# A decoder trunk's attention layer: low parts of weights on VectorE, small multiplications on GpSimd, one transfer for a piece of compression's weights

## The chip, the cores and the metric

The kernel runs on one core of a Trainium2 chip. Its engines run side by side: TensorE (PE: matrix products, and PEld: its weight loads), VectorE (DVE), ScalarE (ACT), GpSimd (POOL), and SyncE (SP), which here only issues transfers. Sixteen DMA engines move data between the chip's memory (HBM) and the engines' buffer (SBUF); products are summed in eight banks of PSUM. The metric is the time of one execution in microseconds (us), the median of several.

## The reference

Two layers over 256 tokens of 1024 channels, float32 throughout. The change lies in the second layer, between the two feed-forward parts:

```python
def compress(kv_raw, pe, w1, w2):
    idx = jnp.arange(n_cmp)[:, None] * D_CMP + jnp.arange(L_CMP)[None, :]      # blocks of 32 tokens, step 16
    blocks = kv_raw[:, idx] + pe[None, None, :, None, :]
    blocks = blocks.transpose(0, 1, 3, 2, 4).reshape(bsz, n_cmp, N_KV_GROUPS, L_CMP * HEAD_DIM)
    return jax.nn.silu(blocks @ w1) @ w2                                       # w1: 2048 x 256

# x: stream after layer 0
kv = (rms_norm(x, kv_norm) @ w_kv).reshape(bsz, seq, 6, 4, 64)   # compressed, selected and window K and V
k_cmp, v_cmp = compress(kv[:, :, 0], ...), compress(kv[:, :, 1], ...)
qg = rms_norm(x, b_norm) @ w_qg                                  # 16 heads' queries, and gates
o = g0 * attend(q, k_cmp, v_cmp) + g1 * attend(q, k_slc, v_slc) + g2 * attend(q, k_win, v_win)
x = x + o @ w_o
x = x + swiglu(rms_norm(x, f_norm)) 
```

Each of the three attentions is a softmax with a distance bias per head. The first layer (a gated short convolution and a feed-forward part) and the last feed-forward part are not touched.

## The kernel before

Tokens lie along the free dimension, channels along the 128 partitions. For accuracy each operand of a product is split into a *high part* (rounded to fp32r) and a *low part* (the rest): `h_...` and `l_...`; a product is then two or three products. So each piece of weights, 128 × 1024, goes through three steps in `split_weights`: SyncE issues its transfer into a raw buffer `w_...` (L316 or L318), ScalarE or GpSimd copies it to `h_...` (L320, L322), VectorE or GpSimd subtracts to `l_...` (L326). The table `CFG["units"]` says for each piece who does it: `False` is ScalarE for the high part and VectorE for the low part; `True` gives the low part to GpSimd; `'both'` gives each half of the low part; `'hi'` gives the high part to GpSimd; `'all'` gives it both parts.

From the attention layer on there are four raw buffers (tag `raw`), so the transfer of a piece waits until the piece four places before it is split; and three buffers for the parts of each of two rings (`a`, `r`).

The pieces of the attention layer are named K (keys; K0 and K1 are what will be compressed), Q, V, Y (`w1` of the compression: Y00 to Y03 for keys, Y10 to Y13 for values), GP (gates) and O (output). `CFG["plan"]` is the order in which the layer is written: `K2a` is the product with that piece, `CB0` builds the blocks `xc` of keys to compress from `cf0` (L767, L768), `Y00` multiplies them with a piece of `w1` into `py` (L779, L780), `J` and `t` are the hidden layer and its transposition, `ck` the compressed keys, `S0` the scores of a head (`sa`, `sb`, L964), and `A`, `r` ask for one more piece ahead. A marker `|n` sets which engines keep the written order from there on; elsewhere a scheduler places instructions by its own costs. From `|4` on no engine is bound, from `|5` TensorE is:

```python
Q0b K4b A Y00 A A A Y10 R0 B1 Y11 A V0 A M0 Y01 A Y02 V1 Y03 J0 Y12 A r A KR4 KR2 A |5 Y13 J1 t0 GP Q1a t1 ck
V2 P0 S0 M1 GR G0 B2 A B3 S1 B4 A C0 S2 V3 G1 B5 N cv A Q1b Q2a r r S3 G2 T0 Q2b R1 ...
```

Products of Y: a piece holds four blocks of 128 rows (two token offsets of 64 channels each) by 256 columns. `CFG["eng"]` names an engine for small steps: `r` scales a head's reciprocal sums by its gates (L988), `c` subtracts a maximum from the compressed scores `cb` (L998), `s` and `m` scale the compressed sums and probabilities (L1008, L1009), `q` splits the queries (first letter high part, second low part; `a`, `d`, `p` are ScalarE, VectorE, GpSimd).

Of the kernel before, what the change touches and what calls it, by code (L numbers as in the profile page):

```python
# [24 lines left out]
DH = 64  # L25
# [24 lines left out]
         'b7': 'p',  # L50
         'b8': 'a',
         'b9': 'p',
         'c0': 'd',
         'c1': 'd',
         'c2': 'd',
         'c3': 'd',
         'c4': 'p',
         'c5': 'p',
         'c6': 'd',
         'c7': 'p',  # L60
         'g000': 'p',
         'g001': 'p',
# [53 lines left out]
         'g900': 'p',  # L116
         'g901': 'p',
         'g910': 'a',
         'm0': 'd',
         'm1': 'd',  # L120
         'm2': 'p',
         'm3': 'p',
         'm4': 'd',
         'm5': 'p',
         'm6': 'p',
         'm7': 'd',
         'q00': 'ap',
         'q01': 'ad',
         'q10': 'pd',
         'q11': 'ad',  # L130
         'q20': 'pd',
         'q21': 'ad',
         'q30': 'pd',
         'q31': 'pp',
         'r0': 'p',
         'r1': 'd',
         'r10': 'd',
         'r11': 'p',
         'r12': 'd',
         'r13': 'p',  # L140
         'r14': 'd',
         'r15': 'p',
         'r4': 'd',
         'r5': 'p',
         'r6': 'd',
         'r7': 'd',
         'r8': 'd',
         'r9': 'p',
         's0': 'p',
         's1': 'd',  # L150
         's2': 'd',
         's3': 'p',
         's4': 'd',
         's5': 'p',
         's6': 'p',
         's7': 'd',
         'x0': 'ap',
         'x1': 'ap',
         'x2': 'pp',
# [9 lines left out]
 'qdma': 0,  # L169
 'sq': {'n1': 0, 'n3': 1},  # L170
 'units': {'GP': ('a', False),
           'K0a': ('a', 'all'),
           'K0b': ('a', False),
           'K1a': ('r', False),
           'K1b': ('r', 'both'),
           'K2a': ('a', 'both'),
           'K2b': ('a', False),
           'K4a': ('a', 'both'),
           'K4b': ('r', 'both'),
           'O0a': ('r', False),  # L180
# [3 lines left out]
           'O2a': ('r', False),
           'O2b': ('r', 'both'),
           'O3a': ('a', 'both'),
           'O3b': ('r', True),
           'O4a': ('r', True),
           'O4b': ('r', True),
           'O5a': ('r', 'both'),  # L190
           'O5b': ('r', True),
           'O6a': ('r', 'both'),
           'O6b': ('a', 'all'),
           'O7a': ('a', 'both'),
           'O7b': ('r', True),
           'Q0a': ('a', 'both'),
           'Q0b': ('r', 'both'),
           'Q1a': ('a', False),
           'Q1b': ('r', 'both'),
           'Q2a': ('a', False),  # L200
           'Q2b': ('a', True),
           'Q3a': ('a', True),
           'Q3b': ('a', True),
           'V0': ('a', True),
           'V1': ('r', 'both'),
           'V2': ('r', False),
           'V3': ('a', True),
           'Y00': ('a', True),
           'Y01': ('a', 'both'),
           'Y02': ('r', False),  # L210
           'Y03': ('a', False),
           'Y10': ('r', True),
           'Y11': ('a', True),
           'Y12': ('a', 'both'),
           'Y13': ('r', 'both')}}
CFG["plan"] = """
H4 K2a H7 K0a A H5 A A K0b A K1a H2 A H0 B0 H1 |4 A K1b H3 NR H6 A A A I NS CR0 CR1 A CB0 K2b Q0a K4a CB1 A
Q0b K4b A Y00 A A A Y10 R0 B1 Y11 A V0 A M0 Y01 A Y02 V1 Y03 J0 Y12 A r A KR4 KR2 A |5 Y13 J1 t0 GP Q1a t1 ck
# [9 lines left out]
def trunk(ctx: ExitStack, tc: tile.TileContext, a):  # L228
    nc = tc.nc
# [32 lines left out]
    def bank(name, kind="short", hold=False):  # L262

        b = min((b for b in ring[kind] if b not in held.values()), key=used.get)
        touch(b)
        if hold:
            held[name] = b
        return psum.tile([P, 512], F32, tag=f"b{b}", name=name)
# [7 lines left out]
    def f(ap):  # L276
        return ap.bitcast(F32)
# [24 lines left out]
    def split_weights(src, name, cols, ring, pool):  # L302
        if (name[0], ring) in spare:
            w, hi, lo = spare.pop((name[0], ring))
        else:
            if phase["name"] == "attention" or name[0] == "O" or name[:2] == "kv":
                w = wp.tile([P, 1024], F32, tag="raw", name=f"w_{name}", bufs=4)
            else:
                w = phase["pool"].tile([P, 1024], F32, tag="raw", name=f"w_{name}", bufs=12)
            hi, lo = (wp.tile([P, 1024], F32R, tag=ring + hl, name=f"{hl}_{name}", bufs=3) for hl in "hl")  # L310
            if name[0] == "O":
                spare[name[0], ring] = [x[:, cols:] for x in (w, hi, lo)]
            w, hi, lo = (x[:, :cols] for x in (w, hi, lo))
        if isinstance(src, list):
            for r, part in enumerate(src):
                nc.sync.dma_start(out=w[r * DH:(r + 1) * DH].rearrange("p (two x) -> p two x", two=2), in_=part)  # L316
        else:
            nc.sync.dma_start(out=w, in_=src)  # L318
        if pool in ("hi", "all"):
            nc.gpsimd.tensor_copy(hi, w)  # L320
        else:
            nc.scalar.activation(hi, w, AF.Copy)  # L322
        cut = {False: 0, True: cols, "both": cols // 2, "hi": 0, "all": cols}[pool]
        for eng, c0, c1 in ((nc.gpsimd, 0, cut), (nc.vector, cut, cols)):
            if c0 < c1:
                eng.tensor_tensor(out=lo[:, c0:c1], in0=w[:, c0:c1], in1=f(hi[:, c0:c1]), op=ALU.subtract)  # L326
        return hi, lo

    class Stream:
# [3 lines left out]
        def ahead(self, n=3):  # L333
            while len(self.ready) < n:
                u = next(self.todo, None)
                if not u:
                    return
                self.ready.append(split_weights(u[1], u[0], u[2], u[4] if len(u) > 4 else self.ring, u[3]))
# [22 lines left out]
    takes = {}  # L361
# [5 lines left out]
    for q in range(4):  # L367
        for st in range(2):

            w1 = a["w1"][st].rearrange("(two d) x -> d two x", two=2)  # L370
            takes[f"Y{st}{q}"] = [w1[:, :, (4 * half + q) * 512:(4 * half + q + 1) * 512] for half in range(2)], 1024
        takes[f"V{q}"] = a["w_v"][q], 1024
    takes["GP"] = a["w_g"], KC * 48

# [395 lines left out]
    def cmp_piece(st, q):  # L770
        if q == 0:
            py[st] = bank(f"py{st}", hold=True)
        wh, wl = wa.take()
        for i in range(4):

            lp = 4 * q + 2 * (i % 2) + i // 2
            first, last = q == 0 and i == 0, q == 3 and i == 3
            x = xc[st].rearrange("p hl g (n l) -> p l (hl g) n", l=16)[:, lp]
            nc.tensor.matmul(py[st][:, :256], x, wh[:, i * 256:(i + 1) * 256], start=first, stop=False)  # L779
            nc.tensor.matmul(py[st][:, :256], x, wl[:, i * 256:(i + 1) * 256], start=False, stop=last)  # L780
# [316 lines left out]
    def hid(st):  # L1097
# [6 lines left out]
          "Q": lambda x: q_piece(int(x[0]), "ab".index(x[1])), "R": lambda x: q_rest(int(x)),  # L1104
          "P": lambda x: q_split(int(x)), "M": lambda x: cmp_second(int(x)),
          "Y": lambda x: cmp_piece(int(x[0]), int(x[1])), "J": lambda x: cmp_hidden(int(x)),
          "V": lambda x: value_piece(int(x)), "N": lambda x: value_rest(), "GP": lambda x: gate_proj(),
          "GR": lambda x: gate_rest(), "B": lambda x: bias(int(x)), "t": lambda x: hid(int(x)),
# [156 lines left out]
```

## Time and profile before

| | before |
|---|---|
| median of 3 runs | 662.78 us (661.78 to 668.63) |
| the profiled execution | 669.47 us, its span 667.6 us |
| TensorE busy | 628.9 us (94%) |
| VectorE busy | 490.3 us (73%) |
| ScalarE busy | 379.1 us (57%) |
| GpSimd busy | 326.0 us (49%) |
| mean granted clock of TensorE | 0.976 of full speed |
| moved by DMA | 109.52 MB, mean 164 GB/s |

The attention layer runs from about 280 to 475 us of the span. A busy share is a mean over stages with different limits; what a change is worth is read from the stage in which it lies.

### The profile page before, as it was taken

To read this page: it belongs to the slowest core of one execution; us is meant where nothing else is said; L and a number is where in the kernel's file an instruction comes from. 1 tells how busy PE (TensorE), PEld (TensorE's weight loads), DVE (VectorE), ACT (ScalarE), POOL (GpSimd) and SP (SyncE) were. 2 spreads that over 40 slices of the span, in tenths; PEclk is the share of its full clock that TensorE was granted. 3 is DMA by queue.
4 is the path that set the end of the run, shared out by engine and by line. 5 is a ranking of instruction groups with operands and counts; after the bars stand their busy time and mean duration, and the time that the engine had idled before them with its cause. 6 is when DMAs were issued, how large, how long until landed. Compare 5 with 4: busy or idle time off the path is not lost.

```text
span 667.6 us, 11200 instructions
## 1 busy us (share of the span) xinstructions
PE 628.9 (94%) x4094; PEld 573.1 (86%) x4094; DVE 490.3 (73%) x773; ACT 379.1 (57%) x744; POOL 326.0 (49%) x285
## 2 busy tenths in 40 slices
PE   7999999999999999879959979999899999999995
PEld 7999998899999999769949869889788888888884
DVE  5688777866666666769996998787986666666664
ACT  7544457545555544437655758997766554444543
POOL 3163225754444444547564675757845444444422
PEclk9999999999999999989989889999899999999998
DMA  8978672655555550031767520003975555555001
GB/s 299 356 303 256 214 245 83 220 190 189 189 187 187 183 179 23 1 127 54 194 171 233 166 95 2 17 17 130 407 291 182 186 179 180 187 186 188 1 1 63
DMA packets 37383, 109.52 MB, mean 164 GB/s; under 512 B 5712, under 2 KB 8144, under 8 KB 37328
## 3 DMA queue, kind: packets, MB, share of 16 engines
q1 hardware_dynamic: 37184, 108.55, 48.0%
q8 instruction: 32, 0.52, 0.3%
q10 hardware_dynamic: 144, 0.26, 0.1%
q14 instruction: 23, 0.19, 0.1%
HBM read 107.22 MB, written 1.05 MB: 162 GB/s over the span
## 4 chain that ended last, share of the span: by engine, by line
PE 75%; DVE 14%; issue 3%; POOL 3%; ACT 3%; DMA 1%; SPq 0%; POOLq 0%; DVEq 0%; ACTq 0%
PE pgu L654 22%; PE pgu L656 11%; PE acc L397 4%; PE acc L398 4%; PE acc L396 4%; PE acc L716 3%; PE acc L715 3%; PE acc L714 3%; DVE n L451 2%; PE pcv L398 2%; PE pcv L397 2%; PE pcv L396 2%; DVE xc L768 1%; POOL l_d L326 1%; PE po L1051 1%
## 5 line engine op out<-in xcount | busy, mean ns | idle before, releaser
L654 PE MATMUL pgu<-n,h_gu 128*128 128x512 f32 x704 | 250.6, 398 | 4.1 <-DVE n L451 2.5
L656 PE MATMUL pgu<-n,l_gu 128*128 128x256 f32 x704 | 197.3, 281 | 0.4 <-DVE l_gu L326 0.4
L654 PEld LDWEIGHTS pgu<-n,h_gu 128*128 128x128 f32 x704 | 132.7, 189 | 35.1 <-DVE n L451 2.5
L326 DVE TENSOR_TENSOR l_gu<-w_gu,h_gu 128x1024 fp32r<-128x1024 f32 x88 | 117.1, 1332 | 26.5 <-ACT h_gu L322 25.4
L656 PEld LDWEIGHTS pgu<-n,l_gu 128*128 128x128 f32 x704 | 133.4, 190 | 2.2 <-DVE l_gu L326 1.1
L667 POOL TENSOR_TENSOR gu<-gu,n_rbc 128x512 f32<-128x512 f32 x40 | 53.2, 1332 | 166.0 <-DVE gu L663 145.1
L672 DVE TENSOR_TENSOR av<-sg,gu 128x256 f32<-128x256 f32 x44 | 79.5, 1809 | 67.9 <-ACT sg L670 67.9
L326 POOL TENSOR_TENSOR l_d<-w_d,h_d 128x1024 fp32r<-128x1024 f32 x43 | 105.2, 2450 | 7.7 <-ACT h_d L322 7.2
L322 ACT ACTIVATE h_gu<-w_gu 128x1024 fp32r<-128x1024 f32 x88 | 92.7, 1053 | 7.1 <-PE pb L397 3.5
L418 ACT ACTIVATE a_h<-av 128x256 fp32r<-128x256 f32 x44 | 18.3, 417 | 78.9 <-DVE av L672 78.9
L322 ACT ACTIVATE h_d<-w_d 128x1024 fp32r<-128x1024 f32 x44 | 46.8, 1063 | 24.5 <-PE acc L716 20.4
L396 PE MATMUL acc<-a_h,h_d 128*128 128x256 f32 x176 | 50.6, 289 | 5.1 <-ACT a_h L418 5.1
L670 ACT ACTIVATE sg<-gu 128x256 f32<-128x256 f32 x44 | 18.2, 417 | 62.1 <-POOL gu L667 52.5
L397 PE MATMUL acc<-a_l,h_d 128*128 128x256 f32 x176 | 50.8, 289 | 0.7 <-DVE a_l L421 0.7
L398 PE MATMUL acc<-a_h,l_d 128*128 128x256 f32 x176 | 50.5, 287 | 0.0
L326 DVE TENSOR_TENSOR l_in<-w_in,h_in 128x768 fp32r<-128x768 f32 (+1 forms) x33 | 38.8, 1187 | 10.7 <-ACT h_in L322 9.5
L322 ACT ACTIVATE h_in<-w_in 128x768 fp32r<-128x768 f32 (+1 forms) x33 | 27.1, 824 | 29.7 <-PE pb L397 20.5
L396 PEld LDWEIGHTS acc<-a_h,h_d 128*128 128x128 f32 x176 | 34.3, 196 | 6.4 <-ACT a_h L418 5.6
L661 ACT ACTIVATE gu<-pgu 128x256 f32<-128x256 f32 x88 | 32.4, 370 | 11.4 <-PE pgu L656 11.4
L398 PE MATMUL pcv<-n,l_in 128*128 128x256 f32 x128 | 36.9, 288 | 1.7 <-DVE l_in L326 1.7
L396 PE MATMUL pcv<-n,h_in 128*128 128x256 f32 x128 | 36.7, 287 | 1.5 <-ACT h_in L322 1.5
L663 DVE TENSOR_TENSOR gu<-pgu,gu 128x256 f32<-128x256 f32 x88 | 36.4, 416 | 1.4 <-ACT gu L661 1.3
(432 smaller groups left out, 1642.1 us busy)
## 6 DMA issues: line engine op xcount, KB each, us to landing
w_gu<-in_w_gu SPq DMA_DIRECT2D x88, 512.0 KB, 4.1
w_d<-in_w_down SPq DMA_DIRECT2D x44, 512.0 KB, 3.4
w_in<-in_w_in SPq DMA_DIRECT2D x31, 384.0 KB, 6.4
w_wo<-in_w_out SPq DMA_DIRECT2D x8, 512.0 KB, 6.7
w_kvY<-in_w SPq DMA_DIRECT2D x16, 256.0 KB, 4.2
w_kvV<-in_w_v SPq DMA_DIRECT2D x4, 512.0 KB, 3.7
h<-in_xT SPq DMA_DIRECT2D x3, 256.0 KB, 5.9
out<-y SPq DMA_DIRECT2D x3, 256.0 KB, 2.3
```

The costliest lines, as they stand in the source:

```text
L322: nc.scalar.activation(hi, w, AF.Copy)
L326: eng.tensor_tensor(out=lo[:, c0:c1], in0=w[:, c0:c1], in1=f(hi[:, c0:c1]), op=ALU.subtract)
L396: nc.tensor.matmul(out, wh, xh, start=start, stop=False, skip_group_check=True)
L397: nc.tensor.matmul(out, wh, xl, start=False, stop=False, skip_group_check=True)
L398: nc.tensor.matmul(out, wl, xh, start=False, stop=stop, skip_group_check=True)
L654: nc.tensor.matmul(ps[j][c], uh[:, cols], x[:, :, k], start=k == 0, stop=False, skip_group_check=True)
L656: nc.tensor.matmul(ps[j][c][:, :S], ul[:, cols], x[:, 0, k], start=False, stop=k == KC - 1, skip_group_check=True)
L661: nc.scalar.activation(gus[j][:, c], ps[j][c][:, S:], AF.Copy)
L663: nc.vector.tensor_tensor(out=gus[j][:, c], in0=ps[j][c][:, :S], in1=gus[j][:, c], op=ALU.add)
L667: (nc.gpsimd if j < NF - 2 else nc.vector).tensor_tensor(out=gu, in0=gu, in1=norm.bc.unsqueeze(1).to_broadcast([P, 2, S]), op=ALU.mult)
L672: nc.vector.tensor_tensor(out=av, in0=sg, in1=gu[:, 1], op=ALU.mult)
L714: nc.tensor.matmul(out, xh, wh, start=start, stop=False, skip_group_check=True)
```

## The change

It has three parts. First, the table `units` gives nearly all low parts of K, Q, V, Y and GP to VectorE and their high parts to ScalarE; most O pieces get `'hi'`, so GpSimd makes the high part and VectorE the low one. Second, the table `eng` gives 21 small steps (five `c`, four `m`, eight `r`, four `s`) from VectorE to GpSimd; q00 and q10 change too. Third, a piece of `w1` comes in one transfer: the rows that a piece takes change (64 of 128 rows of the array, both halves of the columns), and with them the order `lp` in which `cmp_piece` takes its blocks.

```diff
@@ CFG['eng'] @@
-         'c0': 'd',          (c1, c2, c3, c6; m0, m1, m4, m7; r1, r4, r6, r7, r8, r10, r12, r14; s1, s2, s4, s7 alike)
+         'c0': 'p',
-         'q00': 'ap',
+         'q00': 'ad',
-         'q10': 'pd',
+         'q10': 'ad',
@@ CFG['units'] @@
-           'K0a': ('a', 'all'),
+           'K0a': ('a', False),
-           'K1b': ('r', 'both'),          (K2a, K4a, K4b, Q0a, Q0b, Q1b, V1, Y01, Y12, Y13 alike)
+           'K1b': ('r', False),
-           'Y00': ('a', True),            (Q2b, Q3a, Q3b, V0, V3, Y10, Y11 alike)
+           'Y00': ('a', False),
-           'O0b': ('r', 'all'),           (O1a: 'all'; O2a: False; O2b, O3a, O5a, O6a: 'both'; O3b, O4a, O4b, O5b: True)
+           'O0b': ('r', 'hi'),
...
-        if isinstance(src, list):
-            for r, part in enumerate(src):
-                nc.sync.dma_start(out=w[r * DH:(r + 1) * DH].rearrange("p (two x) -> p two x", two=2), in_=part)
-        else:
-            nc.sync.dma_start(out=w, in_=src)
+        nc.sync.dma_start(out=w, in_=src)
...
-            w1 = a["w1"][st].rearrange("(two d) x -> d two x", two=2)
-            takes[f"Y{st}{q}"] = [w1[:, :, (4 * half + q) * 512:(4 * half + q + 1) * 512] for half in range(2)], 1024
+            w1 = a["w1"][st, q % 2 * DH:(q % 2 + 1) * DH].rearrange("d (half x) -> half d x", half=2)
+            takes[f"Y{st}{q}"] = w1[:, :, q // 2 * 1024:(q // 2 + 1) * 1024], 1024
...
-            lp = 4 * q + 2 * (i % 2) + i // 2
+            lp = 8 * (q // 2) + 2 * i + q % 2
```

Code behind these places moves up by four or five lines: L316 and L318 become L314, L326 becomes L322.

SyncE's transfers from Q0b's to GP's, before (`kh` are copies of keys within the buffer):

```order
L318 DMA w_kvQ0b_3643<-in_w_q 128x1024
L318 DMA w_kvK4b_3687<-in_w_kv 128x1024
L316 DMA w_kvY00_3694<-in_w1 64x2x512 x2
L316 DMA w_kvY10_3701<-in_w1 64x2x512 x2
L316 DMA w_kvY11_3719<-in_w1 64x2x512 x2
L318 DMA w_kvV0_3821<-in_w_v 128x1024
L316 DMA w_kvY01_3875<-in_w1 64x2x512 x2
L316 DMA w_kvY02_3892<-in_w1 64x2x512 x2
L318 DMA w_kvV1_3899<-in_w_v 128x1024
L316 DMA w_kvY03_3906<-in_w1 64x2x512 x2
L316 DMA w_kvY12_3934<-in_w1 64x2x512 x2
L316 DMA w_kvY13_3956<-in_w1 64x2x512 x2
```

and with the change:

```order
L314 DMA w_kvQ0b_3639<-in_w_q 128x1024
L314 DMA w_kvK4b_3682<-in_w_kv 128x1024
L314 DMA w_kvY00_3688<-in_w1 128x1x1024
L314 DMA w_kvY10_3694<-in_w1 128x1x1024
L314 DMA w_kvY11_3711<-in_w1 128x1x1024
L314 DMA w_kvV0_3812<-in_w_v 128x1024
L314 DMA w_kvY01_3866<-in_w1 128x1x1024
L314 DMA w_kvY02_3881<-in_w1 128x1x1024
L314 DMA w_kvV1_3887<-in_w_v 128x1024
L314 DMA w_kvY03_3893<-in_w1 128x1x1024
L850 DMA kh_3483<-kh_3483 64x2x256 x2
L314 DMA w_kvY12_3920<-in_w1 128x1x1024
```

Each Y piece is one transfer in place of two, in the same place of the queue; Y13's follows Y12's in both, and two `kh` copies now stand ahead of these two. The pattern shown is the destination's.

VectorE from Q0b's low part to that of Y02, the stretch from about 322 to 345 us, before:

```order
L326 TENSOR_TENSOR l_kvQ0b_3645<-w_kvQ0b_3643,h_kvQ0b_3644 128x512
L483 COPY n2_rbc_3713<-n2_bc_3710 128x256
L752 TENSOR_TENSOR cf0_3715<-pkv0_3525,n2_rbc_3713 128x512
L752 TENSOR_TENSOR cf1_3717<-pkv1_3602,n2_rbc_3713 128x512
L326 TENSOR_TENSOR l_kvK4b_3689<-w_kvK4b_3687,h_kvK4b_3688 128x512
L768 TENSOR_TENSOR xc_3726<-cf0_3715,xc_3726 64x2x240 x4
L768 TENSOR_TENSOR xc_3726<-cf1_3717,xc_3726 64x2x240 x4
L894 SCALAR_TENSOR_TENSOR qf0_3922<-pq0_3761,n2_rbc_3713 128x512
L421 TENSOR_TENSOR w2s_0_3967<-w2_0_3964,w2s_0_3967 128x256
L421 TENSOR_TENSOR q1_0_4183<-qf0_3922,q1_0_4183 64x512
L847 TENSOR_TENSOR keyf4_4039<-pkv4_3786,n2_rbc_3713 128x512
L326 TENSOR_TENSOR l_kvY02_3894<-w_kvY02_3892,h_kvY02_3893 128x1024
```

and with the change, from K4b's low part on:

```order
L322 TENSOR_TENSOR l_kvK4b_3684<-w_kvK4b_3682,h_kvK4b_3683 128x1024
L748 TENSOR_TENSOR cf0_3707<-pkv0_3524,n2_rbc_3705 128x512
L748 TENSOR_TENSOR cf1_3709<-pkv1_3599,n2_rbc_3705 128x512
L322 TENSOR_TENSOR l_kvY00_3690<-w_kvY00_3688,h_kvY00_3689 128x1024
L764 TENSOR_TENSOR xc_3717<-cf0_3707,xc_3717 64x2x240 x4
L764 TENSOR_TENSOR xc_3717<-cf1_3709,xc_3717 64x2x240 x4
L322 TENSOR_TENSOR l_kvY11_3713<-w_kvY11_3711,h_kvY11_3712 128x1024
L889 SCALAR_TENSOR_TENSOR qf0_3908<-pq0_3752,n2_rbc_3705 128x512
L322 TENSOR_TENSOR l_kvV0_3814<-w_kvV0_3812,h_kvV0_3813 128x1024
L322 TENSOR_TENSOR l_kvY10_3696<-w_kvY10_3694,h_kvY10_3695 128x1024
L417 TENSOR_TENSOR w2s_0_3949<-w2_0_3946,w2s_0_3949 128x256
L842 TENSOR_TENSOR keyf4_4021<-pkv4_3777,n2_rbc_3705 128x512
```

Four whole low parts (Y00, Y11, V0, Y10), which GpSimd made, stand between VectorE's other steps, and K4b's is whole.

## Rows read from the trace of the kernel before

**Rows 1.** The page's parts 1 and 4: busy time by engine, the chain by engine.

```profile
PE 628.9 (94%) x4094; PEld 573.1 (86%) x4094; DVE 490.3 (73%) x773; ACT 379.1 (57%) x744; POOL 326.0 (49%) x285
...
PE 75%; DVE 14%; issue 3%; POOL 3%; ACT 3%; DMA 1%; SPq 0%; POOLq 0%; DVEq 0%; ACTq 0%
```

**Rows 2.** TensorE's waits, 280 to 470 us: us in total, times, longest.

```profile
PE sa L964 <- DVE q L421: 4.9, 1, 4.9
PE acc L396 <- ACT a_h L418: 4.5, 1, 4.5
PE py L779 <- DVE keyf L847: 3.9, 1, 3.9
PE py L779 <- ACT h_kvY L322: 2.0, 1, 2.0
```

**Rows 3.** Busy time by stretches; columns as in the first line.

```profile
core 0: us, PE busy (x) PEld busy (x) DVE busy (x) ACT busy (x) POOL busy (x), PEclk, DMA share, GB/s
302.00:328.00 26.00, 25.14 (x208) 24.76 (x208) 25.90 (x36) 16.90 (x32) 17.68 (x18) 1.00 0.47 130
328.00:346.30 18.30, 10.88 (x68) 9.50 (x66) 17.73 (x15) 10.81 (x16) 12.92 (x6) 0.97 0.53 144
346.30:361.00 14.70, 14.65 (x66) 14.23 (x67) 9.80 (x12) 7.59 (x11) 5.91 (x5) 0.81 0.94 249
380.00:397.00 17.00, 12.11 (x113) 11.84 (x111) 15.03 (x37) 11.18 (x30) 13.65 (x19) 0.98 0.34 118
397.00:470.00 73.00, 70.61 (x526) 66.63 (x526) 59.37 (x227) 61.25 (x190) 47.49 (x84) 0.96 0.15 54
475.00:490.00 15.00, 14.96 (x87) 12.73 (x86) 13.04 (x15) 8.69 (x16) 10.67 (x8) 1.00 1.03 409
```

**Rows 4.** VectorE in order of time, 311 to 347 us: start, us, operation.

```profile
314.58 0.68 DVE L326 TENSOR_TENSOR l_kvK1b<-w_kvK1b,h_kvK1b 128x512 fp32r<-128x512 f32 x1
...
318.69 1.78 DVE L326 TENSOR_TENSOR l_kvK4a<-w_kvK4a,h_kvK4a 128x512 fp32r<-128x512 f32 x1
...
326.16 2.70 DVE L768 TENSOR_TENSOR xc<-cf,xc 64x480 fp32r<-64x480 f32 x4
329.18 8.68 DVE L768 TENSOR_TENSOR xc<-cf,xc 64x480 fp32r<-64x480 f32 x4 [0.33 <-ACT xc L767]
```

**Rows 5.** VectorE in order of time, 385 to 395 us.

```profile
385.81 3.43 DVE L326 TENSOR_TENSOR l_O2b<-w_O2b,h_O2b 128x256 fp32r<-128x256 f32 x1
...
392.57 2.17 DVE L998 TENSOR_TENSOR cb<-cb,cm 128x64 f32<-128x64 f32 x1
```

**Rows 6.** GpSimd in order of time, 332 to 388 us.

```profile
332.20 2.42 POOL L326 TENSOR_TENSOR l_kvY<-w_kvY,h_kvY 128x1024 fp32r<-128x1024 f32 x1 [1.06 <-ACT h_kvY L322]
...
385.32 2.41 POOL L326 TENSOR_TENSOR l_kvQ3a<-w_kvQ3a,h_kvQ3a 128x1024 fp32r<-128x1024 f32 x1
```

**Rows 7.** VectorE's groups of one line and shape, 311 to 323 us: busy, mean ns.

```profile
L326 DVE TENSOR_TENSOR l_kvK2b<-w_kvK2b,h_kvK2b 128x1024 fp32r<-128x1024 f32 x1 | 1.2, 1212 | 0.0
```

**Rows 8.** Line L316, which issues compression's weights: ns min/median/max, first and last start.

```profile
L316 SPq DMA_DIRECT2D w_kvY<-in_w x16: 595/600/630, 318.5 to 346.4; - x16
...
DMA to landing us min/median/max: 3.7/4.2/6.3
```

**Rows 9.** The page's part 5: ScalarE's 1024-column high parts.

```profile
L322 ACT ACTIVATE h_gu<-w_gu 128x1024 fp32r<-128x1024 f32 x88 | 92.7, 1053 | 7.1 <-PE pb L397 3.5
```

**Rows 10.** TensorE in order of time, 360 to 362 us.

```profile
360.90 0.39 PE L779 MATMUL py<-h_kvY,xc 128*128 128x256 f32 x1
361.12 0.39 PE L780 MATMUL py<-l_kvY,xc 128*128 128x256 f32 x1
```

**Rows 11.** The page's part 3: the main DMA queue, its share of sixteen engines' span.

```profile
q1 hardware_dynamic: 37184, 108.55, 48.0%
```

**Rows 12.** Line L998, the `cb` sum, on both engines: ns min/median/max.

```profile
L998 DVE TENSOR_TENSOR cb<-cb,cm x5: 221/226/2174, 380.9 to 445.9; 128x64 f32<-128x64 f32 x5
L998 POOL TENSOR_TENSOR cb<-cb,cm x3: 292/292/292, 429.7 to 453.5; 128x64 f32<-128x64 f32 x3
```

More of the change, by code (lines that the diff above doesn't have):

```diff
@@ L52 @@
          'b9': 'p',
[L53 to L56, printed above, removed]
+         'c0': 'p',
+         'c1': 'p',
+         'c2': 'p',
+         'c3': 'p',
          'c4': 'p',
          'c5': 'p',
-         'c6': 'd',
+         'c6': 'p',
          'c7': 'p',
@@ L118 @@
          'g910': 'a',
-         'm0': 'd',
-         'm1': 'd',
+         'm0': 'p',
+         'm1': 'p',
          'm2': 'p',
          'm3': 'p',
-         'm4': 'd',
+         'm4': 'p',
          'm5': 'p',
          'm6': 'p',
-         'm7': 'd',
-         'q00': 'ap',
+         'm7': 'p',
+         'q00': 'ad',
          'q01': 'ad',
-         'q10': 'pd',
+         'q10': 'ad',
          'q11': 'ad',
@@ L135 @@
          'r0': 'p',
-         'r1': 'd',
-         'r10': 'd',
+         'r1': 'p',
+         'r10': 'p',
          'r11': 'p',
-         'r12': 'd',
+         'r12': 'p',
          'r13': 'p',
-         'r14': 'd',
+         'r14': 'p',
          'r15': 'p',
-         'r4': 'd',
+         'r4': 'p',
          'r5': 'p',
-         'r6': 'd',
-         'r7': 'd',
-         'r8': 'd',
+         'r6': 'p',
+         'r7': 'p',
+         'r8': 'p',
          'r9': 'p',
          's0': 'p',
-         's1': 'd',
-         's2': 'd',
+         's1': 'p',
+         's2': 'p',
          's3': 'p',
-         's4': 'd',
+         's4': 'p',
          's5': 'p',
          's6': 'p',
-         's7': 'd',
+         's7': 'p',
          'x0': 'ap',
@@ L171 @@
  'units': {'GP': ('a', False),
-           'K0a': ('a', 'all'),
+           'K0a': ('a', False),
            'K0b': ('a', False),
            'K1a': ('r', False),
-           'K1b': ('r', 'both'),
-           'K2a': ('a', 'both'),
+           'K1b': ('r', False),
+           'K2a': ('a', False),
            'K2b': ('a', False),
-           'K4a': ('a', 'both'),
-           'K4b': ('r', 'both'),
+           'K4a': ('a', False),
+           'K4b': ('r', False),
            'O0a': ('r', False),
-           'O0b': ('r', 'all'),
-           'O1a': ('r', 'all'),
+           'O0b': ('r', 'hi'),
+           'O1a': ('r', 'hi'),
            'O1b': ('r', 'hi'),
[L184 to L192, printed above, removed]
+           'O2a': ('r', 'hi'),
+           'O2b': ('r', 'hi'),
+           'O3a': ('a', 'hi'),
+           'O3b': ('r', 'hi'),
+           'O4a': ('r', 'hi'),
+           'O4b': ('r', 'hi'),
+           'O5a': ('r', 'hi'),
+           'O5b': ('r', 'hi'),
+           'O6a': ('r', 'hi'),
            'O6b': ('a', 'all'),
@@ L195 @@
            'O7b': ('r', True),
-           'Q0a': ('a', 'both'),
-           'Q0b': ('r', 'both'),
+           'Q0a': ('a', False),
+           'Q0b': ('r', False),
            'Q1a': ('a', False),
-           'Q1b': ('r', 'both'),
+           'Q1b': ('r', False),
            'Q2a': ('a', False),
[L201 to L205, printed above, removed]
+           'Q2b': ('a', False),
+           'Q3a': ('a', False),
+           'Q3b': ('a', False),
+           'V0': ('a', False),
+           'V1': ('r', False),
            'V2': ('r', False),
-           'V3': ('a', True),
-           'Y00': ('a', True),
-           'Y01': ('a', 'both'),
+           'V3': ('a', False),
+           'Y00': ('a', False),
+           'Y01': ('a', False),
            'Y02': ('r', False),
            'Y03': ('a', False),
[L212 to L215, printed above, removed]
+           'Y10': ('r', False),
+           'Y11': ('a', False),
+           'Y12': ('a', False),
+           'Y13': ('r', False)}}
 CFG["plan"] = """
```

## The prediction

> **What bounds the kernel now.** I read the page's busy table and its chain of waits first, then TensorE's waits, then busy time by stretches, then the operations named there. TensorE is busy for 94% of the span and holds 75% of the chain [rows 1]: time can be won only where it stands still or is slowed. Of its stops in the part that the change touches, four carry 15.3 us: 4.5 for the last feed-forward tile, 3.9 and 2.0 at the compression products, 4.9 before a score product [rows 2]. The stretches say the same: from 328.0 to 346.3 us TensorE is busy for 10.9 of 18.3, from 380 to 397 for 12.1 of 17, and from 397 to 470 it misses 2.4 of 73 [rows 3]. In those stretches VectorE is nearly full (25.9 of 26.0, 17.7 of 18.3): there it is the bound, and what it does counts in full.
>
> VectorE is full partly because its instructions are stretched. The four `xc` subtractions of cf0 took 2.70 us, the four equal ones of cf1 8.68; a 512-column low part took 0.68 us once and 1.78 another time; a 64-column `cb` sum took 2.17 [rows 4, 5]. Each long one lies beside a low part on GpSimd, where 1024 columns take 2.4 us [rows 6]. A full 1024-column low part on VectorE takes 1.21 [rows 7]. So a low part that is shared between both can hold VectorE longer than the whole would alone.
>
> **The change, part by part.** The profiled execution took 669.47 us (span 667.6 and 1.9 around it), 6.7 above the median of 662.78; the sum is made on it, and 6.7 is taken off at the end.
>
> *Low parts at 281 to 294 us.* K0a's and K2a's go to VectorE; K0a's high part goes to ScalarE. It adds 1.2 us and half of another to VectorE, and takes GpSimd's subtraction out of the way of the tile whose end TensorE awaits for 4.5. Bounds: +1.2 (nothing is unstretched), −4.5 (the wait is gone). I take −2, between them, since VectorE's own added work eats part.
>
> *Low parts at 311 to 346 us.* VectorE takes five halves more (5 × (1.21 − 0.68) = 2.7), four full parts ahead of `keyf2` (4 × 1.21 = 4.8), half of Y01 (0.5) and q0_0 (as an equally large 512-column one, 0.7): 8.7 us. It loses the stretching: 8.68 − 2.70 = 6.0 on `xc` and 1.78 − 0.68 = 1.1 on K4a, 7.1 us in these rows alone, more where others are stretched. About even: bounds +1.6 to −3.9, the whole wait for `keyf2`. Were the weights there as early as now, I would take −3.9, for the `xc` rows are the largest. They aren't, as follows.
>
> *Compression's weights as one transfer.* Now each of the eight 512-KB pieces comes in two transfers, each of 64 rows by two runs of 2 KB (16 of them, the first issued at 318.5 us, the last at 346.4 [rows 8]). Their stretch has a DMA share of 0.94 [rows 3]: with the pattern 64, 2, 512 all sixteen engines work. The new pattern of the source is 2, 64, 1024: its outermost count is 2, since the rearrangement puts `half` first; the order shows the destination as 128 rows. How a transfer is dealt out to the engines when its outermost count is below sixteen, no row shows: every transfer of the kernel has 64 or 128 there. Two ends, then. If it is cut by runs, all sixteen share it and the price is 0. If it is cut along the outermost dimension, there are two shares and two engines carry it, 262,144 bytes each. One engine moves 409 / (16 × 1.03) = 24.8 GB/s where all are full, from 475 to 490 us [rows 3]; that is 10.6 us for a piece. I take the second: each count that the trace has splits evenly over sixteen along its outermost dimension, and 2 doesn't.
>
> The Trainium skill says the same of the hardware: "DMA: Bandwidth & Descriptors", "Why a DMA increments its semaphore by 16 and not by 1", has the number of engines follow from the slowest dimension, of more than one element, of both patterns, as the largest number up to 16 that divides both; 2 and 128 give 2 here. It speaks against this change, which otherwise has fewer and longer runs. No run here has shown it; by its opposite the sum would be that of the first rival.
>
> Now the price on the path. SyncE's queue has Y00, Y10, Y11, V0, Y01, Y02, V1, Y03, Y12, Y13 in that order, and each waits for the raw buffer of the fourth before it. The first goes out at 318.5 − 2 (the earlier stage) = 316.5. Landing costs 3.7 (the shortest of before, for 256 KB) less 0.7 for its bytes on sixteen engines = 3.0 [rows 8]. On the two engines the eight pieces stand one behind the other: 8 × 10.6 = 84.8; V0's and V1's shares, 32 KB on each engine, add 2 × 1.3. The queue doesn't run dry: Y00 lands at 330 and its buffer is free at 332.5, while Y10 and Y11 keep the engines until 351; later ones likewise. The last piece lands at 316.5 + 3.0 + 84.8 + 2.6 = 406.9; its high part (1.1 [rows 9]), its low part (1.2) and its eight products, 0.22 apart, end at 411. Now the last one ends at 361.5 [rows 10]: **+49.5 us**. Nothing covers it: from Y13 on TensorE keeps the plan's order, and t0, GP, Q1a, ck and all scores stand behind Y13; V2 and V3 wait for raw buffers of Y12 and Y13, and VectorE has Y12 and Y13 ahead of y0. The −3.9 above is swallowed, for TensorE then waits for weights. Bounds: −1 (eight issues of 0.6 us fewer on a queue that isn't the bound), and 10.6 replaced by 12.4, from the mean of the span (108.55 MB in 48.0% of sixteen engines × 667.6 us = 21.2 GB/s [rows 11]), which adds 14. TensorE may come back at a low clock: after the stop at 346 it had 0.81 for 14.7 us [rows 3], 2.8 us lost; twice that is 5.6.
>
> *The rest.* Q3a, Q3b, O1b and O2b at 378 to 397 us: +3.4 us on VectorE (2 × 1.21, 0.68 and 0.3), against 3.43 − 0.4 and 2.17 − 0.2 of stretching [rows 5] (a 256-column part without company is estimated at 0.4 from the 0.68 of 512). The `sa` product waits 4.9 there: bounds +1 to −4.9, taken −2. The small multiplications: 21 move, four to 64 columns each; one costs 0.29 us on GpSimd for 0.22 to 0.23 on VectorE [rows 12], so 21 × 0.2 = 4 us leave VectorE, and O3 to O6's low parts bring about as much back. Each adds a hand-over between the engines, but 1 to 2 steps ahead of its use. TensorE misses only 2.4 us in that stretch: 0, bounds ±2.
>
> Sum: 669.5 + 49.5 − 2 = 717; the −2 of the first stage is already in the 316.5. On the scale of the median 717 − 6.7 = **710**.
>
> **Rivals.** *A, faster:* the transfers are shared by all sixteen. Then nothing of the 49.5 exists, and the stages give −2 − 3.9 − 2 = −8: 655, at best 650. For it: the rows of 4 KB are longer than now and the bytes the same. Against: a first count of 2. It decides at eight shares: then a piece takes 2.6 us, the eight 21, less than the 28 us over which they are issued now, and nothing is late. *B, VectorE gains nothing:* shared by all sixteen, but the stretching stays, since GpSimd still has copies and small multiplications there; then the 8.7 and 3.4 us stand against nothing and, less the 4.0 that leave, add up to 8: 663 to 671. Against it: between 311 and 346 GpSimd is left with two fills and little else. *C, slower still:* the two engines are also slow (12.4 us a piece) and TensorE comes back at a low clock (0.81 is between its levels of 1.2 and 2.4 GHz): 710 + 14 + 5.6 = 730.
>
> **How the numbers follow.** Two engines (with C): 0.83, own range 702 (the better bounds of the other stages) to 732; A: 0.10; B: 0.07, half of it within 1%. About 1% is what a measurement of this kernel tells from no change. Slower 0.86, same 0.05, faster 0.09. To hold 8 in 10 the range must take in nearly all of the first case, so some 5 us more at each end: 697 to 737. Most chance lies with one sign, and the range doesn't reach to A.
>
> **What would show it.** A DMA share near 2/16 = 0.13 from about 320 to 400 us; `w_kvY` eight times, 512 KB, 13 us and more to landing, up to 30 with the queue; TensorE waiting for `h_kvY` or `l_kvY` by 40 to 60 us in all; the last `py` product at 405 to 425 us; `xc` at 0.66 to 0.7 each; the wait at 289 us shorter than 4.5. I am wrong if a piece lands in 4 to 6 us at a share above 0.5; then the time is A's or B's. If pieces take 13 us but the end moves by much less than 40, some work behind Y13 has passed it.

## The result, and the profile after

The changed kernel takes 712.1 us (median of 6 runs, 710.6 to 713.2) where the one before takes 665.6 (6 runs beside it, 661.8 to 669.5): a ratio of 1.070, 95% interval 1.064 to 1.075. It is slower by 46 us; 710 was forecast. The kernel before takes near 662 us in some executions and near 668 in others. The profiled execution took 710.58 us, with a span of 708.8.

The page's parts 1 and 4 of the changed kernel, the answer to [rows 1]:

```profile
PE 628.2 (89%) x4094; PEld 568.7 (80%) x4094; DVE 475.8 (67%) x768; ACT 375.7 (53%) x737; POOL 288.0 (41%) x282
...
PE 61%; DMA 18%; DVE 9%; ACT 3%; POOL 3%; issue 3%; SPq 1%; POOLq 0%; ACTq 0%; DVEq 0%
PE pgu L650 19%; DMA w_kvY<-in_w 11%; PE pgu L652 10%; PE acc L393 3%; PE acc L394 3%; PE acc L392 3%; PE acc L712 3%; PE acc L711 3%; PE acc L710 3%; DMA w_gu<-in_w_gu 2%; DMA w_in<-in_w_in 1%; DVE av L668 1%; PE pcv L394 1%; PE pcv L392 1%; PE pcv L393 1%
```

TensorE is as busy as before (628.2 us, 628.9 before), VectorE less (475.8 for 490.3), GpSimd much less (288.0 for 326.0). All that was moved did come off those engines, and the span grew. The new item is DMA: 18% of the chain for 1%, of which 11%, 78 us, are the transfers of `w_kvY`.

Part 2, where each digit is a tenth of an engine's time in a slice of 17.7 us:

```profile
PE   7999999999999998995324499999699999999995
...
PEclk9999999999999999997556599999999999999998
DMA  8986744655555610332211553000894655556101
```

From the 19th slice (319 us) TensorE falls to 2 to 5 tenths for 89 us, and for 71 of them DMA has 1 or 2: both are idle at once. A busy table alone would call nothing the bound. The stretches, to be laid against [rows 3]:

```profile
core 0: us, PE busy (x) PEld busy (x) DVE busy (x) ACT busy (x) POOL busy (x), PEclk, DMA share, GB/s
...
302.00:328.00 26.00, 23.91 (x196) 23.50 (x196) 18.17 (x29) 13.01 (x20) 6.47 (x5) 1.00 0.35 111
328.00:346.30 18.30, 2.10 (x9) 1.80 (x9) 3.82 (x6) 3.05 (x5) 0.00 (x0) 0.54 0.13 52
346.30:361.00 14.70, 8.11 (x20) 5.31 (x20) 6.09 (x8) 3.15 (x5) 0.00 (x0) 0.50 0.26 80
361.00:380.00 19.00, 3.71 (x13) 3.12 (x14) 4.31 (x6) 4.50 (x6) 0.53 (x1) 0.50 0.18 63
380.00:397.00 17.00, 10.02 (x41) 8.60 (x40) 3.97 (x7) 2.33 (x5) 0.53 (x1) 0.70 0.43 124
410.00:430.00 20.00, 20.00 (x157) 18.57 (x156) 18.59 (x59) 15.36 (x45) 9.95 (x18) 1.00 0.52 176
```

From 328 to 346 us the sixteen engines have a share of 0.13 = 2/16, and 52 GB/s pass: two engines at 26 GB/s each. With sixteen at work the stretch that followed had 0.94 and 249 GB/s [rows 3]. Who pays is in TensorE's waits, 280 to 480 us (us in total, times, longest), to be laid against [rows 2]:

```profile
PE py L774 <- ACT h_kvY L318: 31.0, 5, 8.5
PE pval L864 <- ACT h_kvV L318: 16.2, 1, 16.2
PE py L775 <- DVE l_kvY L322: 2.8, 4, 0.8
...
PE pTc L1027 <- POOL pcp L1004: 1.4, 1, 1.4
PE acc L392 <- ACT a_h L414: 1.3, 1, 1.3
```

31.0 and 2.8 us at the compression's products, and 16.2 more at a product with V, whose 512 KB stand behind three pieces in the same queue. The old stops are gone or small: `keyf` (3.9) and `q` (4.9) aren't in the list, `a_h` has fallen from 4.5 to 1.3. But ScalarE only hands on what it was made to wait for. Its own copies, start, us, and in brackets the idle time before:

```profile
322.71 1.06 ACT L318 ACTIVATE h_kvY<-w_kvY 128x1024 fp32r<-128x1024 f32 x1 [8.47 <-DMA w_kvY<-in_w]
343.67 1.06 ACT L318 ACTIVATE h_kvY<-w_kvY 128x1024 fp32r<-128x1024 f32 x1 [15.02 <-DMA w_kvY<-in_w]
345.90 1.04 ACT L318 ACTIVATE h_kvY<-w_kvY 128x1024 fp32r<-128x1024 f32 x1
355.90 1.06 ACT L318 ACTIVATE h_kvY<-w_kvY 128x1024 fp32r<-128x1024 f32 x1 [7.48 <-DMA w_kvY<-in_w]
365.99 1.06 ACT L318 ACTIVATE h_kvY<-w_kvY 128x1024 fp32r<-128x1024 f32 x1 [9.03 <-DMA w_kvY<-in_w]
...
389.05 1.06 ACT L318 ACTIVATE h_kvY<-w_kvY 128x1024 fp32r<-128x1024 f32 x1 [7.71 <-DMA w_kvY<-in_w]
400.64 1.06 ACT L318 ACTIVATE h_kvY<-w_kvY 128x1024 fp32r<-128x1024 f32 x1 [10.53 <-DMA w_kvY<-in_w]
```

From the third copy on a piece comes every 10 to 11.7 us. The last product with `w1` ends at 404.9, where [rows 10] has 361.5:

```profile
404.51 0.43 PE L775 MATMUL py<-l_kvY,xc 128*128 128x256 f32 x1
```

From there to the end of the span it is 303.9 us, before 306.1: the whole loss lies ahead of this product. VectorE meanwhile works as the change means it to; this is the answer to [rows 4], all eight `xc` subtractions as one entry at 0.68 us each, where the last four alone took 8.68:

```profile
324.94 5.44 DVE L764 TENSOR_TENSOR xc<-cf,xc 64x480 fp32r<-64x480 f32 x8
```

### The profile page after: what moved, and what is told of

Same layout as the page of the kernel before. It is cut to its first block, busy times and chain, and to the rows that moved or that the text cites. A ratio compares the mean times of both kernels' runs of the same rounds, so it can differ in the third digit from the quotient of the medians.

```text
span 708.8 us, 11139 instructions
## 1 busy us (share of the span) xinstructions
PE 628.2 (89%) x4094; PEld 568.7 (80%) x4094; DVE 475.8 (67%) x768; ACT 375.7 (53%) x737; POOL 288.0 (41%) x282
## 4 chain that ended last, share of the span: by engine, by line
PE 61%; DMA 18%; DVE 9%; ACT 3%; POOL 3%; issue 3%; SPq 1%; POOLq 0%; ACTq 0%; DVEq 0%
PE pgu L650 19%; DMA w_kvY<-in_w 11%; PE pgu L652 10%; PE acc L393 3%; PE acc L394 3%; PE acc L392 3%; PE acc L712 3%; PE acc L711 3%; PE acc L710 3%; DMA w_gu<-in_w_gu 2%; DMA w_in<-in_w_in 1%; DVE av L668 1%; PE pcv L394 1%; PE pcv L392 1%; PE pcv L393 1%
## 5 line engine op out<-in xcount | busy, mean ns | idle before, releaser
L322 DVE TENSOR_TENSOR l_gu<-w_gu,h_gu 128x1024 fp32r<-128x1024 f32 x88 | 119.6, 1361 | 28.6 <-ACT h_gu L318 27.5
L668 DVE TENSOR_TENSOR av<-sg,gu 128x256 f32<-128x256 f32 x44 | 81.6, 1855 | 68.3 <-ACT sg L666 68.3
L322 POOL TENSOR_TENSOR l_d<-w_d,h_d 128x1024 fp32r<-128x1024 f32 x43 | 105.0, 2443 | 18.3 <-ACT h_d L318 17.9
L318 ACT ACTIVATE h_gu<-w_gu 128x1024 fp32r<-128x1024 f32 x88 | 92.7, 1054 | 11.0 <-PE pgu L650 3.9
L318 ACT ACTIVATE h_d<-w_d 128x1024 fp32r<-128x1024 f32 x44 | 46.9, 1065 | 22.6 <-PE acc L712 17.5
L322 DVE TENSOR_TENSOR l_kvY<-w_kvY,h_kvY 128x1024 fp32r<-128x1024 f32 x8 | 9.8, 1225 | 62.3 <-ACT h_kvY L318 62.3
L393 PE MATMUL acc<-a_l,h_d 128*128 128x256 f32 x176 | 49.5, 282 | 0.4 <-DVE a_l L417 0.4
L322 DVE TENSOR_TENSOR l_in<-w_in,h_in 128x768 fp32r<-128x768 f32 (+1 forms) x33 | 38.8, 1188 | 10.2 <-ACT h_in L318 9.0
L318 ACT ACTIVATE h_kvY<-w_kvY 128x1024 fp32r<-128x1024 f32 x8 | 8.4, 1055 | 67.7 <-DMA w_kvY<-in_w 67.7
L774 PE MATMUL py<-h_kvY,xc 128*128 128x256 f32 x32 | 13.9, 441 | 32.8 <-ACT h_kvY L318 31.0
L318 ACT ACTIVATE h_in<-w_in 128x768 fp32r<-128x768 f32 (+1 forms) x33 | 27.2, 826 | 29.3 <-PE pb L393 21.8
L774 PEld LDWEIGHTS py<-h_kvY,xc 128*128 128x128 f32 x32 | 10.0, 314 | 35.1 <-ACT h_kvY L318 33.0
```

Source lines behind the costliest of these rows:

```text
L393: nc.tensor.matmul(out, wh, xl, start=False, stop=False, skip_group_check=True)
L668: nc.vector.tensor_tensor(out=av, in0=sg, in1=gu[:, 1], op=ALU.mult)
```

## The experiments

Twelve kernels. Medians in us; ratios to the kernel before with their 95% intervals.

| run | median | ratio | interval |
|---|---|---|---|
| the change | 712.1 | 1.070 | 1.064 to 1.075 |
| two_transfers | 651.1 | 0.980 | 0.976 to 0.984 |
| plain_one | 651.5 | 0.980 | 0.974 to 0.986 |
| eight_shares | 657.3 | 0.991 | 0.987 to 0.995 |
| four_shares | 673.5 | 1.013 | 1.008 to 1.018 |
| before_one | 716.4 | 1.078 | 1.073 to 1.083 |
| before_units | 657.5 | 0.988 | 0.984 to 0.993 |
| before_eng | 664.4 | 0.998 | 0.995 to 1.002 |
| before_first | 655.0 | 0.986 | 0.983 to 0.990 |
| before_rest | 661.4 | 0.997 | 0.993 to 1.000 |
| two_old_eng | 656.9 | 0.989 | 0.983 to 0.994 |
| late_gp_new_eng | 654.5 | 0.984 | 0.979 to 0.989 |
| late_gp_old_eng | 653.8 | 0.983 | 0.978 to 0.988 |

**Is it the pattern's outermost count?** Theory: two elements there, so two engines. First rival: one transfer per piece, or the longer rows, or the other order of blocks costs the time. *two_transfers* keeps rows and order, but sends each half by itself, so that 64 rows stand outermost:

```diff
-        nc.sync.dma_start(out=w, in_=src)
+            for r, part in enumerate(src):
+                nc.sync.dma_start(out=w[r * DH:(r + 1) * DH], in_=part)
-            takes[f"Y{st}{q}"] = w1[:, :, q // 2 * 1024:(q // 2 + 1) * 1024], 1024
+            takes[f"Y{st}{q}"] = [w1[half, :, q // 2 * 1024:(q // 2 + 1) * 1024] for half in range(2)], 1024
```

> The changed kernel, but each piece of compression's weights comes in two transfers of 64 rows by one run of 4 KB, outermost count 64. Shares theory (a transfer uses as many DMA engines as its outermost count allows: 2): the 46 us vanish, pieces land in 4 to 6 us, 650 to 660 us. VectorE theory (the loss comes from the low parts moved to VectorE): 700 to 712 us. Runs theory (the 4-KB runs or the rows chosen are slow to read): 700 to 712 us, pieces still land 10 us apart.

61 us come back, and the kernel is faster than both. Its view of the tile `w_kvY` (the issues, and for how long an engine stood idle until a transfer landed):

```profile
L316 SPq DMA_DIRECT2D w_kvY<-in_w x16: 465/574/590, 309.3 to 334.0; - x16
...
  DMA w_kvY<-in_w: 5.0, 4
```

In the changed kernel that idle time is 67.7 us in 7 times. Rows and order of blocks are cleared; the number of transfers isn't yet. *plain_one* is one transfer of 128 whole rows, outermost count 128; the products are then made with other weights.

```diff
-            w1 = a["w1"][st, q % 2 * DH:(q % 2 + 1) * DH].rearrange("d (half x) -> half d x", half=2)
-            takes[f"Y{st}{q}"] = w1[:, :, q // 2 * 1024:(q // 2 + 1) * 1024], 1024
+            w1 = a["w1"][st]
+            takes[f"Y{st}{q}"] = w1[:, q * 1024:(q + 1) * 1024], 1024
```

> The changed kernel, but a piece is 128 whole rows of 1024 neighbouring columns, one transfer with outermost count 128; the rows meet other blocks, so the compressed keys and values are computed from other weights. Shares theory: sixteen engines, 650 to 653 us; one transfer against two is worth nothing, since the queue that issues them has room. If one transfer is itself what costs: over 700 us.

One transfer of 512 KB costs nothing. *four_shares* and *eight_shares* change the count alone (4 × 32 × 1024 and 8 × 16 × 1024 elements, other weights as well):

```diff
+            w1 = a["w1"][st, q * 32:(q + 1) * 32].rearrange("d (four x) -> four d x", four=4)
+            takes[f"Y{st}{q}"] = w1, 1024
```
```diff
+            w1 = bass.AP(w1.tensor, w1.offset + q * 1024, [[15 * 4096, 8], [4096, 16], [1, 1024]])
```

> The changed kernel, but the source pattern of a piece is 4, 32, 1024 in place of 2, 64, 1024; it takes other rows of the array, so the compressed keys and values are computed from other weights; bytes and instructions are the same. Shares theory: four engines, 131,072 bytes each, at 26 GB/s 5.0 us a piece, eight of them 40 us and not 81; the last piece lands about 40 us earlier than with two shares, at 355 to 362 us, and the time is 658 to 672 us. Runs theory: no different from two shares, 705 to 715 us.

> The changed kernel, but the source pattern of a piece is 8, 16, 1024; it takes other, partly repeated rows of the array, so the compressed keys and values are computed from other weights; bytes and instructions are the same. Shares theory: 65,536 bytes on each of eight engines, 2.5 us a piece at 26 GB/s, 20 us for eight, less than the 25 us over which two_transfers issues them: 650 to 656 us, as two_transfers. A theory in which any pattern with the halves or blocks outermost is slow to read: over 660 us.

Counts 2, 4, 8 and 64 or 128 give 712.1, 673.5, 657.3 and 651: the time falls with each doubling, both middle runs somewhat above what was expected. TensorE's waits with four shares:

```profile
PE py L774 <- ACT h_kvY L318: 9.5, 3, 4.2
PE pval L864 <- ACT h_kvV L318: 4.4, 1, 4.4
```

The same two waits, at 13.9 in place of 47.2 us. Where little else was moved, its engines had a share of 0.26 = 4/16, and 103 GB/s passed, 26 for each of four:

```profile
322.00:328.00 6.00, 5.11 (x36) 4.91 (x35) 3.75 (x6) 2.11 (x4) 0.00 (x0) 1.00 0.26 103
```

The Trainium skill's rule ("DMA: Bandwidth & Descriptors", "Why a DMA increments its semaphore by 16 and not by 1") agrees with all five: the shares of 0.13 and 0.26 in the traces are its two and four engines out of sixteen. Only the source's count was varied; the destination has 64 or 128 rows in all five.

**The parts alone, on the kernel before.** *before_one* has the transfer alone, *before_units* the table `units`, *before_eng* the table `eng`; each is the change's own lines of that part.

> The kernel before with the transfer part of the change alone (pattern 2, 64, 1024 and the order of blocks that goes with it). Shares theory: 665.6 + 45 to 55 = 710 to 720 us, pieces land 10 to 11 us apart. VectorE theory: 663 to 670 us.

> The kernel before with the table of weights alone (low parts of K, Q, V, Y, GP and O to VectorE). If the stretching of VectorE's instructions beside GpSimd's goes: 655 to 662 us against 665.6 for the kernel before. If VectorE is merely loaded more: 668 to 678 us.

> The kernel before with the small multiplications on GpSimd alone. The prediction's 0 within 2: 661 to 665 us against 663.1 for the kernel before. If the hand-overs between the engines cost: over 667 us; if VectorE's relief counts in full: 657 to 660 us.

The transfer is worth +7.8% by itself, the low parts −1.2%, the small multiplications nothing. Why nothing, TensorE's waits of *before_eng* from 300 to 470 us say:

```profile
PE pTc L1032 <- POOL pcp L1009: 3.9, 1, 3.9
```

The 4.9 of `sa` behind `q` are gone (part of them belonged to that execution, for *before_first* below, with the same code there, waits 1.1), 3.9 at `pcp` are new, for GpSimd now owes that small product and has this ahead of it:

```profile
384.50 2.41 POOL L326 TENSOR_TENSOR l_kvQ3a<-w_kvQ3a,h_kvQ3a 128x1024 fp32r<-128x1024 f32 x1
...
387.71 2.36 POOL L326 TENSOR_TENSOR l_kvQ3b<-w_kvQ3b,h_kvQ3b 128x1024 fp32r<-128x1024 f32 x1
390.14 1.11 POOL L843 CAST vc<-vc 64x1024 fp32r<-64x1024 f32 x1
...
392.50 0.29 POOL L1009 TENSOR_TENSOR pcp<-cb,cs 128x64 f32<-128x64 f32 x1
```

**Are the small multiplications worth something once GpSimd is free of low parts?** *two_old_eng* is *two_transfers* with the table `eng` of before. *late_gp_new_eng* and *late_gp_old_eng* are *two_transfers* and *two_old_eng* with Q2b's, Q3a's, Q3b's and the O pieces' entries of before, which gives those low parts back to GpSimd.

```diff
-           'Q3a': ('a', False),          (Q2b, Q3b alike; from 'hi': O3b, O4a, O4b, O5b to True, O2b, O3a, O5a, O6a to 'both', O0b, O1a to 'all', O2a to False)
+           'Q3a': ('a', True),
```

> The changed kernel with two transfers for a piece and the small multiplications where the kernel before has them (VectorE and GpSimd). If moving them to GpSimd is worth 4 us or more of VectorE's time in the scores: 655 to 658 us, as before_units. If it is worth nothing (the prediction's 0, within 2): 649 to 653 us, and the 6 us between before_units and two_transfers come from the transfers' longer runs.

> The fastest kernel so far (the change, with a piece of w1 in two transfers of 64 rows by 4 KB, ratio 0.980) with Q2b's, Q3a's, Q3b's and the O pieces' entries of the table of units as before, so that GpSimd has low parts to make at 378 to 420 us, beside the small multiplications. Theory: the small multiplications help only where GpSimd isn't busy with low parts; here they stand behind them and TensorE waits for pcp for 3 us or more, in place of 1.4; ratio 0.986 to 0.994. Rival: what GpSimd has at that time doesn't matter; ratio 0.978 to 0.983.

> The same with the table of small steps (eng) of before as well. Theory: with low parts on GpSimd the small multiplications are worth nothing on either engine, so the time is that of the run beside it within 0.4%: ratio 0.986 to 0.994. Rival: the small multiplications on GpSimd are worth 0.9% whatever else GpSimd does (as measured without those low parts): 0.7% or more slower than the run beside it.

Without late low parts on GpSimd the table is worth 5.8 us (656.9 to 651.1; the single runs, 654.1 to 659.0 and 650.5 to 653.0, don't overlap); with them nothing (653.8 and 654.5). The wait for `pcp` is 3.9 again in *late_gp_new_eng*, as the theory had it, though both times came out shorter than expected. So neither move brings anything by itself there: taking the late low parts off GpSimd alone gives 656.9 for 653.8, with intervals that overlap, moving the small multiplications alone 654.5; both together give 651.1.

**Where do the low parts earn their 1.2%?** *before_first* changes two entries of before alone, K0a and K2a; *before_rest* all the others of the part.

```diff
-           'K0a': ('a', 'all'),
+           'K0a': ('a', False),
-           'K2a': ('a', 'both'),
+           'K2a': ('a', False),
```

> The kernel before with two entries of its table of units changed alone: K0a and K2a with the low part on VectorE and the high part on ScalarE. Theory: GpSimd's subtractions for these two pieces stretch VectorE's steps ahead of the last feed-forward tile; without them TensorE's stop there falls from 4.5 us to about 1.3, the product that ends layer 0 ends near 296 us and the first transfer of compression's weights goes out near 310 us, not 318.5. The time falls by 3 us or more: ratio 0.990 to 0.996, and no less than two thirds of what all the units gave (0.988). Rival 1 (the prediction's step): the gain at this place is about 2 us, first such transfer near 316.5, ratio 0.996 to 1.000. Rival 2: the earlier transfers only bring TensorE sooner to the wait for keyf2 and the stretched subtractions at 326 to 338 us: first transfer near 310, the wait there longer, ratio 0.998 to 1.003.

> The kernel before with all changes of the table of units except K0a and K2a. Theory: the stop of 4.5 us at the last feed-forward tile stays and the first transfer of compression's weights stays near 318.5 us; the four equal xc subtractions of cf1 take 0.65 to 0.7 us each in place of 2.2, and the wait for keyf2 (3.9 us) goes; since the weights are no earlier, TensorE waits for them instead by 2 us or more. Ratio 0.994 to 1.000. Rival 1: the unstretched VectorE is what counts and not the first stage: ratio 0.986 to 0.991, as with all units. Rival 2: gains add up without touching each other: the two runs' gains sum to that of all the units (1.2%) within 0.4%.

The two entries bring 1.4% (1.0 to 1.8%), at the end all that the part brings; the others 0.35%. The stretch from 285 to 302 us, before and then with the two entries:

```profile
285.00:302.00 17.00, 12.08 (x77) 11.58 (x76) 11.15 (x14) 6.69 (x15) 6.36 (x4) 0.80 0.29 104
```
```profile
285.00:302.00 17.00, 15.64 (x129) 15.24 (x128) 15.48 (x23) 11.42 (x27) 10.34 (x12) 1.00 0.29 95
```

TensorE does 129 products for 77, and the granted clock is 1.00 for 0.80. VectorE's product by `n_rbc` ahead of the awaited tile, before and with the two entries:

```profile
290.10 2.56 DVE L667 TENSOR_TENSOR gu<-gu,n_rbc 128x512 f32<-128x512 f32 x1
```
```profile
286.08 0.69 DVE L667 TENSOR_TENSOR gu<-gu,n_rbc 128x512 f32<-128x512 f32 x1
```

In *before_rest* the stop stays (4.6 us), `xc` is as short as in the changed kernel, and at the end nearly nothing is gained:

```profile
PE acc L396 <- ACT a_h L418: 4.6, 1, 4.6
```
```profile
323.14 5.44 DVE L768 TENSOR_TENSOR xc<-cf,xc 64x480 fp32r<-64x480 f32 x8
```

On the way there it was another picture. *before_units* differs from *before_first* by the other entries alone, and in both layer 0 ends at 295.7 us. The last product with `w1`, with the other entries and without:

```profile
346.97 0.38 PE L780 MATMUL py<-l_kvY,xc 128*128 128x256 f32 x1
```
```profile
352.65 0.39 PE L780 MATMUL py<-l_kvY,xc 128*128 128x256 f32 x1
```

There the other entries are 5.7 us ahead; at the end of the span (656.3 and 652.9) they are 3.4 behind. TensorE's waits behind that product, with them and without:

```profile
PE sa L964 <- DVE q L421: 4.2, 1, 4.2
PE pgu L654 <- DVE n L451: 4.2, 1, 4.2
PE pgu L656 <- DVE l_gu L326: 2.0, 1, 2.0
```
```profile
PE pgu L654 <- DVE n L451: 2.0, 2, 1.5
PE sa L964 <- DVE q L421: 1.1, 1, 1.1
```

The wait for `n`, at the first tile of the last feed-forward part, goes with the late low parts: it is 4.9 and 4.6 in *two_transfers* and *two_old_eng*, 2.5 and 2.6 in the two kernels that give those back to GpSimd. What holds VectorE up there was not tried.

## Why the prediction was right, step by step

**What bounds the kernel.** Held: TensorE's stops set the time, and those named went as said; what took their place is the transfer.

**One transfer.** The mechanism is shown: two engines, 26 GB/s each for the 24.8 that were taken. From the first issue to the last landing 316.5 to 406.9, 90.4 us, were worked out; the changed kernel has 309.8 (the first issue) to 400.6 (ScalarE starts on the last piece), 90.9. That these agree so well is luck: at 26 GB/s the eight pieces take 80.7 us and not 84.8, but the last two come 11.3 and 11.6 us apart, the fifth 10.1 after the fourth, and the sum has nothing for that. The price by itself, *before_one*, is 7.8% of 663 us, 51.5 us (48 to 55), for 49.5. In the changed kernel, against *two_transfers*, it is 61 us: there the pieces would otherwise be multiplied by 346.0, and the two engines' 91 us are a floor that gives nothing back for earlier work. The part spoke of this for the `keyf` wait alone ("swallowed"); it holds for all that is won between the first issue and Y13.

**Low parts at 281 to 294 us.** Right in kind, mis-sized: −2 was taken, first issue at 316.5; it came at 309.8, 8.7 us earlier than before, past the lower bound of −4.5. The term counted the stop alone, and took part of that away for VectorE's added work. The stop fell by 3.2 (4.5 to 1.3), the added work cost nothing (the product by `n_rbc` fell by 1.9), and the low clock after the stop was left out: at 0.80 for 17 us a fifth of the stretch, 3.4 us, is lost, and that is back too. Most of the rest lies between the end of layer 0 and the first issue, 15.5 us before and 13.7 in the changed kernel: *before_rest* has 13.7 as well and *before_first* 15.4, so this is the later entries' doing. That low parts on GpSimd cause the stop, *before_first* shows.

**Low parts at 311 to 346 us.** "About even" was the term; *before_rest*, which holds the later ones as well, gives −2.3 us (−0.3 to −4.4). That hides a term that was mis-sized: up to the last product with `w1` the later entries gain 5.7 us (*before_units* against *before_first*, which keeps the whole wait for `keyf` and has the four `xc` of cf1 at 8.70 us), more than the −3.9 that an early weight was to leave. The stretched rows did pay at their place; in the changed kernel the transfer swallows it, and in *before_rest* and *before_units* it is lost again at `q`, `n` and `l_gu`.

**The rest.** Q3a to O2b −2 and the small multiplications 0 ± 2 were taken; from the last product with `w1` to the end the time fell by 2.2. That is luck too. Up to the last product with O it fell by 6.3, but *before_first*, with nothing changed there, has the same fall (106.9 us before, 100.6 and 100.5), so it is not shown to be the change's. And behind it stands a loss that the sum doesn't have, TensorE's waits at the start of the last feed-forward part, where before there are 2.0 for `n` alone:

```profile
PE pgu L650 <- DVE n L447: 4.9, 1, 4.9
PE pgu L652 <- DVE l_gu L322: 1.7, 1, 1.7
```

The low parts of O were set against the small multiplications by VectorE's busy time, and not by what waits for VectorE at the end of the layer. The 0 is what *before_eng* measured, but for the wrong reason: the table is worth 5.8 us where GpSimd is free, which the change sees to. "1 to 2 steps ahead of its use" held only then.

**The sum.** 717 less 6.7 for the scale of the median. That 710 lies within 2 us of 712.1 is luck: two errors of near one size cancel. The first stage gave 6.7 more than forecast, and the changed kernel's profiled execution lay 1.5 us below its median (710.6 and 712.1), so that the 6.7 for the scale was not to be taken off. What made the profiled execution of before long lies largely between the last product with `w1` and the last with O; there, before and in *before_first*, with the same code:

```profile
361.50:468.40 106.90, 99.29 (x741) 93.33 (x740) 89.49 (x306) 84.29 (x252) 69.46 (x110) 0.95 0.23 80
```
```profile
353.00:453.60 100.60, 95.81 (x741) 89.57 (x740) 87.15 (x306) 83.81 (x252) 70.78 (x110) 1.00 0.25 87
```

The granted clock is 0.95 and 1.00, and the wait of `sa` for `q` 4.9 and 1.1.

**Rivals.** A, all sixteen shared, is what *two_transfers* is: 651 for 655, "at best 650"; the first stage gave more than its −2, and from the end of layer 0 to the last product with `w1` it takes 50.3 us, *before_first* 57.3, so that the wait for `keyf` did pay there; 2.9 of it go again at `n` (4.9 for 2.0). That it decides at eight shares was nearly right: eight cost 6 us still. B fell: the rows that it kept stretched aren't, `xc` takes 0.68 each. C's slow engines fell with 26 GB/s; its low clock is there, 0.50 to 0.70 from 346 to 397, but TensorE mostly waits then. From 404.9 to 410 it is busy throughout at 0.71, which loses 1.5 us of the 5.6 taken, and from 410 it has 1.00:

```profile
404.90:410.00 5.10, 5.10 (x34) 4.79 (x34) 2.35 (x5) 4.58 (x8) 0.00 (x0) 0.71 0.94 335
```

Of the signs, TensorE's wait for the pieces was too high (40 to 60 forecast, 33.8): the 16.2 at V's product were not foreseen at that place, and with them it is 50.

## What to carry to other kernels

Before a transfer is merged or its source rearranged, read the outermost count of both patterns (here only the source's was varied): with 2, 4 and 8 there the kernel took 712, 673 and 657 us, with 64 or 128 651, and since the transfers queue behind each other, the price is that of the whole series, not of one. When several edits come in one change, look for the small one that undoes the others: here a rearranged view hid a gain of 2%. A helper engine that shares bulk work should not also owe small results to the critical path; move both or neither. Where an edit seems to bring nothing, compare the times at which the stages end: here it won 5.7 us in one and lost them in the next.

## What the runs showed that was not expected

- Two of 31 table entries carry the gain of all, since what the others win up to the last product with `w1` is lost behind it. A stop of 4.5 us cost TensorE 3.4 more, since the granted clock was 0.80 over the 17 us around it; with a stop of 1.3 it was 1.00.
- With eight shares the last piece is copied 14 us after that of *two_transfers* (353.1 and 339.3 us). Of these 2.6 are there at the first issue (311.9 and 309.3), in a profiled execution that was the longest of ten, and the last piece is issued 7.4 us later (341.4 and 334.0); by bytes its share would take no more than 2.6 us. Whether the rest is landing time or buffers coming free later was not tried.
